# Down projection of the second FFN in Strassen's form, with its staging tiles, operand tiles and evacuations laid out anew

## The chip, the cores and the metric

The kernel runs on one core of a Trainium2 chip. The core has five engines that run side by side, each through its own list of instructions in order: TensorE (PE, matrix products, with weight loads shown as PEld), VectorE (DVE), ScalarE (ACT), GpSimd (POOL) and SyncE (SP, which only starts transfers). They share the on-chip memory SBUF; TensorE writes its sums to PSUM, from which VectorE and ScalarE read. The metric is the device time of one execution in microseconds (us), the median of several; lower is better.

## The reference

Two layers of an encoder on one sequence of 1024 tokens with 1024 channels, in float32. What matters here is the second feed-forward block and the norm behind it:

```python
def swiglu_ffn(h, w_gate, w_up, w_down):
    return (jax.nn.silu(h @ w_gate) * (h @ w_up)) @ w_down

for layer in range(DEPTH):
    h = rmsnorm(x, norm_mix_g[layer])
    ...
    x = x + y
    h = rmsnorm(x, norm_ffn_g[layer])
    x = x + swiglu_ffn(h, ffn_w_gate[layer], ffn_w_up[layer], ffn_w_down[layer])
return rmsnorm(x, final_g)
```

The hidden width is 2816, which is 22 chunks of 128. The down projection multiplies the hidden activations (2816 by 1024 tokens) by weights of 2816 by 1024.

## The kernel before

Channels lie on the 128 partitions, tokens along the free dimension, so a matmul takes 128 rows of weights and up to 512 tokens. The precision of float32 is kept by splitting each operand into a rounded part and the rest (`split`, lines 86 to 88): ScalarE casts the rounded part (L87), VectorE subtracts (L88), both from one raw tile to a "hi" and a "lo" tile. A product is then three matmuls (`mm3`, L100 to L102: hi by hi, hi by lo, lo by hi), added up in one PSUM bank.

The feed-forward block of a layer has two stages.

Gate and up (`gate_up_first`, `prep`, `gate_up_rest`, `gate_up_all`) uses Winograd's form of Strassen's products: two chunks of the hidden width, two halves of the channels and two halves of the tokens make a 2 by 2 block product with seven multiplications in place of eight. A pair of chunks has a unit for the gate and a unit for up. VectorE forms the left operands (sums of weight blocks), and the evacuations of the banks combine the products. `fin` applies silu to the gate and multiplies it with up; the four quadrants of the result leave for DRAM (`a_dram`) through GpSimd's queue of transfers.

The down projection (`down`, L737) is a plain product. It takes one half of the tokens after the other; the hidden chunks come in groups of 8, 7 and 7. For a group the activations are read back and split (`load_a`, L708), one tile of the pool tag "big" each. For each of eight output chunks a weight tile is read and split (`load_w`, L108), the products of the group are added up in one bank (`down_one`), and VectorE adds the bank to the residual `xs[m]` (L726). For layer 1 the second half of the tokens runs in blocks of 256 columns, and in its last group block after block, so that the final norm of the first block runs behind the products of the second. `final` (L876) squares and adds the channels, takes the mean by a matmul with a constant (`norm`, L531), three steps of a root, and writes eight scaled chunks out.

The order of the instructions is set by a planner: it goes through the program with a priority in the order in which the code is written, estimates when each instruction could run, and writes a list for each engine. On the chip each list runs in that order, with waits. Tiles come from pools by tag with a fixed number of buffers, and a new tile waits until an old one of its tag is no longer used. The tags that matter: "big" (28 tiles: residual and right operands), "w" (10: split weights), "raw" (3: weights as read), "cvp" (4), "cv" and "pr" (2 each), "half" (6), "ln" (4), and the PSUM tags "ps" (4 banks), "lnp" (2) and "acc" (2 in one tile). `run_behind` lets VectorE work of a generator be written between products against a budget of us.

Of the kernel before, what the change touches and what calls it, by code (L numbers as in the profile page):

```python
# [16 lines left out]
P = 128  # L17
S = 1024
# [24 lines left out]
def trunk(ctx: ExitStack, tc: tile.TileContext, xT, vecs, cw, w_in, w_out, fmap, pmap,  # L43
          wg, wu, wd, cen_m, pcnt, dft_h, dft_l, seq_h, seq_l, out):
# [20 lines left out]
    STT = nc.vector.scalar_tensor_tensor  # L65

# [15 lines left out]
    # the Newton step below leaves -2 / sqrt(v); the gains carry the -1/2  # L82
# [9 lines left out]
    def paced(ins, rows):  # L92
        """Hold ins until the products have come to that many rows."""
# [11 lines left out]
    def wtile(name):  # L105
        return arena.tile([P, 1024], F32R, tag="w", name=name, bufs=10)

    def load_w(src, cols=1024, eng=None, q=nc.sync, alloc=wtile, rows=None):  # L108
        raw = arena.tile([P, 1024], F32, tag="raw", name="raw", bufs=3)
# [10 lines left out]
    def rsqrt2(ps, e, y, v):  # L120
        """v = -2 / sqrt(ps + eps)"""
# [95 lines left out]
    def make_tables():  # L217
        # per-head feature transform folded with the head's map: [S, C, -S, -C] @ map
# [17 lines left out]
    def load_halves(src, q):  # L236
        raw = arena.tile([P, 1024], F32, tag="raw", name="raw", bufs=3)
        wh, wl = wtile("wh"), wtile("wl")
        for hs in HALVES:
            q.dma_start(raw[:, hs], src[:, hs])  # L240
        return raw, wh, wl
# [34 lines left out]
    # ---- the convolution runs behind the products: chunk 0 and part of chunk 3 on ACT and Pool,  # L276
    # the rest on DVE in what time the products leave it
# [99 lines left out]
    def tick(used):  # L377
        """After a unit of products, in which DVE has that many us of its own."""
# [41 lines left out]
    for h in range(4):  # L420
# [5 lines left out]
        # radix-4 step over the sequence: s = 256 a + b  # L426
# [15 lines left out]
    # W[c][b, (r|i), e] per head, then the 256-point transforms over b  # L442
# [86 lines left out]
    a_dram = [[dram.tile([P, S], F32, name=f"a{layer}_{f}") for f in range(NF)] for layer in range(2)]  # L529

    def norm(lo, hi):  # L531
        """-2 / rms of xs over its columns lo..hi"""
# [8 lines left out]
    # gate and up: Winograd's form of Strassen's products over two chunks of the hidden width (1, 2),  # L541
    # the two halves of the channels and the two halves of the tokens
# [5 lines left out]
    def product(ps, w, b, start, stop):  # L548
        for j in range(4):
            c = j * P  # L550
            mm3(ps, (w[:, c:c + P], w[:, TH + c:TH + c + P]), (b[j][:, :TH], b[j][:, TH:]),
                start and j == 0, stop and j == 3, skip_group_check=not start)
# [35 lines left out]
    def raw_w(src):  # L588
        raw = arena.tile([P, 1024], F32, tag="raw", name="raw", bufs=3)
# [387 lines left out]
```

## Time and profile before

| what | value |
|---|---|
| median of 3 runs | 1744.99 us (1744.05 to 1747.76) |
| span of the profiled execution | 1740.6 us |
| time of the profiled execution beyond its span | not given apart; the median of the runs is 4.4 us longer |
| mean granted TensorE clock | 0.991 |
| moved by DMA | 238.66 MB, 137 GB/s over the span |
| TensorE busy from 1204 to 1455 us (gate and up, layer 1) | 251.00 of 251 us |
| VectorE busy from 1480 to 1602 us (down, first half of the tokens) | 68.47 of 122 us |
| VectorE busy from 1602 to 1730 us (down, second half) | 73.65 of 128 us |
| GpSimd's longest group | 96 additions of 128x512, 139.3 us, all before 280 us |

The profile is one execution, recorded instruction by instruction. In its rows an engine is followed by the line of the kernel, the operation, the tile written and the tiles read, and the shape. A row of the timeline begins with the start and the duration in us, and a bracket at its end gives the time the engine was idle before it and what ended that. A row of the groups gives busy time and the mean of one instruction in ns, then the idle time ahead of the group. A row of the windows gives, for a stretch of time, how long each engine was busy in it.

### The profile page before, as it was taken

The page shows a single profiled execution, that of the slowest core. Times are in us where ns is not written, and L with a number is a line of the kernel's source. Part 1 is how long each engine was busy: PE and PEld are TensorE (multiplying, and loading weights), DVE is VectorE, ACT ScalarE, POOL GpSimd, SP SyncE. Part 2 cuts the span into 40 slices and gives each one's busy share as a digit, 9 for nine tenths or more (in the row PEclk, how much of TensorE's full clock was granted, in tenths as well). Part 3 has the DMA queues.
Part 4 walks back from the last instruction along what each step waited for, and adds up shares of the span by engine and source line. Part 5 has one row for each costly group of instructions (what it writes and reads, how often), then busy time and mean ns, then how long its engine had stood idle before and what let it go on. Part 6 is the DMA issues. An engine that isn't in the chain of part 4 may idle for free.

```text
span 1740.6 us, 22375 instructions
## 1 busy us (share of the span) xinstructions
PE 1682.0 (97%) x8318; PEld 1400.9 (80%) x8318; DVE 1245.9 (72%) x1774; ACT 692.9 (40%) x1062; POOL 276.0 (16%) x300
## 2 busy tenths in 40 slices
PE   6998899999999999999999998999999999999997
PEld 4786777777888888889998886778888888788997
DVE  8699988794577777755559768787777775545546
ACT  5455855464323232233234344553232322334223
POOL 4587764111000000000000001110000000000000
PEclk9999899999999999999999999999999999999999
DMA  5121311545633333355433425646333333644433
GB/s 188 47 97 37 135 61 46 184 142 201 232 131 122 127 109 127 116 167 174 133 109 126 152 85 182 211 163 218 133 122 127 109 127 121 204 144 160 167 122 123
DMA packets 82236, 238.66 MB, mean 137 GB/s; under 512 B 10320, under 2 KB 15696, under 8 KB 82128
## 3 DMA queue, kind: packets, MB, share of 16 engines
q1 hardware_dynamic: 65520, 186.64, 32.6%
q0 software_dynamic: 14304, 47.46, 7.2%
q10 hardware_dynamic: 2304, 3.15, 0.5%
q8 instruction: 65, 1.06, 0.3%
q14 instruction: 43, 0.35, 0.1%
HBM read 190.02 MB, written 47.19 MB: 136 GB/s over the span
## 4 chain that ended last, share of the span: by engine, by line
PE 83%; DVE 11%; DMA 3%; ACT 1%; issue 1%; SPq 0%; DVEq 0%; ACTq 0%
PE ps L100 18%; PE ps L102 18%; PE ps L101 18%; PE lnp L100 10%; PE lnp L102 10%; PE lnp L101 9%; DVE acc L313 2%; DVE acc L134 1%; DMA xin<-in_xT 1%; DMA raw<-in_wd 1%; DVE hl L88 1%; DMA raw<-in_wu 1%; DVE wl L88 1%; DVE ybl L88 0%; PE lnp L538 0%
## 5 line engine op out<-in xcount | busy, mean ns | idle before, releaser
L87 ACT CAST hl<-raw 128x512 fp32r<-128x512 f32 x264 | 161.2, 621 | 426.0 <-DVE raw L636 161.4
L100 PE MATMUL ps<-hl 128*128 128x512 f32 x704 | 277.6, 395 | 3.3 <-ACT s L617 2.8
L102 PE MATMUL ps<-hl 128*128 128x512 f32 x704 | 276.6, 393 | 0.0
L101 PE MATMUL ps<-hl 128*128 128x512 f32 x704 | 276.5, 393 | 0.0
L87 ACT CAST wh<-raw 128x896 fp32r<-128x896 f32 (+2 forms) x139 | 132.5, 953 | 243.5 <-PE ps L101 109.0
L100 PE MATMUL ps<-ahl,wh 128*128 128x256 f32 (+3 forms) x711 | 228.0, 321 | 0.5 <-ACT wh L87 0.5
L102 PE MATMUL ps<-ahl,wl 128*128 128x256 f32 (+3 forms) x711 | 227.7, 320 | 0.5 <-DVE wl L88 0.5
L101 PE MATMUL ps<-ahl,wh 128*128 128x256 f32 (+3 forms) x711 | 227.2, 320 | 0.0
L88 DVE TENSOR_TENSOR hl<-raw,hl 128x512 fp32r<-128x512 f32 x264 | 179.8, 689 | 47.9 <-ACT hl L87 43.3
L100 PE MATMUL lnp<-hl 128*128 128x512 f32 x528 | 210.2, 398 | 0.7 <-ACT s L617 0.7
L102 PE MATMUL lnp<-hl 128*128 128x512 f32 x528 | 208.1, 395 | 0.0
L101 PE MATMUL lnp<-hl 128*128 128x512 f32 x528 | 207.9, 394 | 0.0
L88 DVE TENSOR_TENSOR wl<-raw,wh 128x896 fp32r<-128x896 f32 (+2 forms) x127 | 141.6, 1116 | 48.7 <-ACT wh L87 44.3
L100 PEld LDWEIGHTS ps<-hl 128*128 128x128 f32 x704 | 132.2, 188 | 37.7 <-ACT s L617 6.9
L102 PEld LDWEIGHTS ps<-hl 128*128 128x128 f32 x704 | 132.3, 188 | 30.6
L101 PEld LDWEIGHTS ps<-hl 128*128 128x128 f32 x704 | 132.4, 188 | 29.6
L303 POOL TENSOR_TENSOR cvp<-cvp,pr 128x512 f32<-128x512 f32 x96 | 139.3, 1452 | 82.5 <-ACT pr L302 78.2
L100 PEld LDWEIGHTS ps<-ahl,wh 128*128 128x128 f32 x711 | 134.3, 189 | 11.1 <-ACT wh L87 0.9
L102 PEld LDWEIGHTS ps<-ahl,wl 128*128 128x128 f32 x711 | 134.0, 189 | 10.9 <-DVE wl L88 1.0
L101 PEld LDWEIGHTS ps<-ahl,wh 128*128 128x128 f32 x711 | 134.3, 189 | 10.2 <-issue 0.2
L653 POOL DMA_DIRECT2D a<-g x66 | 35.6, 540 | 576.6 <-DVE g L652 576.6
L100 PEld LDWEIGHTS lnp<-hl 128*128 128x128 f32 x528 | 99.5, 189 | 27.3 <-ACT s L617 4.3
(209 smaller groups left out, 3095.9 us busy)
## 6 DMA issues: line engine op xcount, KB each, us to landing
raw<-in_wg SPq DMA_DIRECT2D x66, 512.0 KB, 3.4
raw<-in_wu SPq DMA_DIRECT2D x66, 512.0 KB, 3.6
raw<-in_wd SPq DMA_DIRECT2D x72, 448.0 KB, 3.3
a<-g POOLq DMA_DIRECT2D x88, 256.0 KB, 3.1
raw<-in_wd SPq DMA_DIRECT2D x32, 512.0 KB, 3.8
p<-s POOLq DMA_DIRECT2D x44, 256.0 KB, 3.2
u<-p SPq DMA_DIRECT2D x44, 256.0 KB, 4.2
raw<-a SPq DMA_DIRECT2D x44, 256.0 KB, 3.3
```

The source lines that it names most:

```text
L87: nc.scalar.copy(hi, src)
L88: (eng or nc.vector).tensor_tensor(out=lo, in0=src, in1=hi.bitcast(F32), op=ALU.subtract)
L100: nc.tensor.matmul(ps, lh, rh, start=start, stop=False, **kw)
L101: nc.tensor.matmul(ps, lh, rl, start=False, stop=False, **kw)
L102: mm = nc.tensor.matmul(ps, ll, rh, start=False, stop=stop, **kw)
L134: TT(out=acc, in0=acc, in1=sq, op=ALU.add)
L303: nc.gpsimd.tensor_tensor(out=a, in0=a, in1=pr, op=ALU.add)
L313: STT(out=acc, in0=src, scalar=wv, in1=acc, op0=ALU.mult, op1=ALU.add)
L653: nc.gpsimd.dma_start(a_dram[layer][m][:, HALVES[t]], dst)
```

## The change

The down projection of layer 1 becomes a 2 by 2 block product of its own, over pairs of hidden chunks (11), pairs of output chunks (j = 0 to 3) and the two halves of the tokens, with seven multiplications. Layer 0 keeps the plain form.

The right operands are made once, at the end of each pair in gate and up: `combine` (called behind the up unit) reads the quadrant B11 back from DRAM, forms T1 to T4 by four additions of 128x512 on GpSimd, and stores them; B11, B21, B22 and T1 to T4 lie in `b_dram`, and B12 is no longer stored.

`down_strassen` runs two passes over blocks of pairs. Pass A has blocks of 2, 3, 3 and 3 pairs; in each block and each j five products run: A11 with B11, S2 with T2, S3 with T3, A12 with B21, A22 with T4. Pass B has blocks of 4, 3 and 4 pairs and two products: S1 with T1 and S4 with B22. Left operands are made anew for each step (`left_a`, `left_b`), one step ahead, by three additions on GpSimd each, then split by ScalarE and VectorE into tiles of tag "w". Both passes read all weights. The right operands of a block are read and split over the four steps of the block before, through the small tags "cv" and "pr", into tiles of tag "big".

Evacuations in pass A: the first product's bank is copied by ScalarE and added by GpSimd to a running sum `u2[j]` (in the first block VectorE adds the copy and the second product directly), the second product's bank is added by VectorE, two banks are copied by ScalarE and added to the residual by GpSimd (`add_pool`), one is added by VectorE. In the last block `u2[j]` is added to three quadrants, two on GpSimd and one on VectorE. In pass B VectorE adds both banks. The final norm runs over whole halves of the tokens: the first behind pass B, the second behind the end.

For the whole kernel the tags "raw" (3) and "w" (10) become one tag "w" of 13 buffers, for raw and split weights alike.

```diff
     def wtile(name):
-        return arena.tile([P, 1024], F32R, tag="w", name=name, bufs=10)
+        return arena.tile([P, 1024], F32R, tag="w", name=name, bufs=13)
+
+    def rawtile():
+        return arena.tile([P, 1024], F32, tag="w", name="raw", bufs=13)
...
+    def combine(p, g):
+        g11 = arena.tile([P, TH], F32, tag="cv", name="g11", bufs=2)
+        nc.sync.dma_start(g11, b_dram["B11"][p])
+        t1, t3 = g11, g["12"]
+        t2, t4 = (arena.tile([P, TH], F32, tag="pr", name=n, bufs=2) for n in ("t2", "t4"))
+        PTT(out=t1, in0=g["12"], in1=g11, op=ALU.subtract)
+        PTT(out=t2, in0=g["22"], in1=t1, op=ALU.subtract)
+        PTT(out=t3, in0=g["22"], in1=g["12"], op=ALU.subtract)
+        PTT(out=t4, in0=g["21"], in1=t2, op=ALU.subtract)
+        for name, src in (("T1", t1), ("T2", t2), ("T3", t3), ("T4", t4)):
+            store_b(1, name, p, src)
...
+    def load_b(names):
+        out = []
+        for n, p in names:
+            bturn[0] += 1
+            tag = ("cv", "pr")[bturn[0] % 2]
+            raw = arena.tile([P, TH], F32, tag=tag, name=tag, bufs=2)
+            nc.sync.dma_start(raw, b_dram[n][p])
+            out.append(opnd(raw, big))
+        return out
...
+    def left_a(j, p0, n):
+        a11, a12, a21, a22 = load_quads(j, p0, n)
+        w = {"A11": wopnd(a11)}
+        s3 = small("s3")[:, :n * P]
+        PTT(out=s3, in0=a11, in1=a21, op=ALU.subtract)
+        PTT(out=a21, in0=a21, in1=a22, op=ALU.add)
+        PTT(out=a21, in0=a21, in1=a11, op=ALU.subtract)
+        w["S2"], w["S3"], w["A12"], w["A22"] = wopnd(a21), wopnd(s3), wopnd(a12), wopnd(a22)
+        return w
...
+        w = left(0)
+        b = right(0, load_b(right_names(0)[1]))
+        for k in range(KD):
+            xs[k] = big(f"x{k}")
+            nc.sync.dma_start(xs[k], x_dram[layer][k])
...
+        def add_pool(dst, ps):
+            t = half("u1")
+            nc.scalar.copy(t, ps)
+            PTT(out=dst, in0=dst, in1=t, op=ALU.add)
...
+        for i, (kind, p0, n, j) in enumerate(steps):
+            if j == 0 and i + 4 < len(steps):
+                todo, got = right_names(i + 4)[1], []
+            nw = left(i + 1) if i + 1 < len(steps) else None
+            (x11, x12), (x21, x22) = x[j]
+            if kind == "a":
+                ba, bb, bd = single(), single(), single()
+                product(ba, w["A11"], b["B11"], True, True)
+                u = half("u1")
+                nc.scalar.copy(u, ba)
+                product(bb, w["S2"], b["T2"], True, True)
+                if u2[j] is None:
+                    u2[j] = arena.tile([P, TH], F32, tag="cvp", name="uu", bufs=4)
+                    TT(out=u2[j], in0=bb, in1=u, op=ALU.add)
+                else:
+                    PTT(out=u2[j], in0=u2[j], in1=u, op=ALU.add)
+                    TT(out=u2[j], in0=bb, in1=u2[j], op=ALU.add)
+                product(bd, w["S3"], b["T3"], True, True)
+                add_pool(x22, bd)
+                product(ba, w["A12"], b["B21"], False, True)
+                add_pool(x11, ba)
+                product(bd, w["A22"], b["T4"], False, True)
+                TT(out=x21, in0=bd, in1=x21, op=ALU.add)
+                if (p0, n) == blocks_a[-1]:
+                    TT(out=x21, in0=x21, in1=u2[j], op=ALU.add)
+                    for dst in (x12, x22):
+                        PTT(out=dst, in0=dst, in1=u2[j], op=ALU.add)
...
-    down(1, ([(0, TH)], [(TH, TH + 256), (TH + 256, S)]), final)
+    down_strassen(1, ((0, 2), (2, 3), (5, 3), (8, 3)), ((0, 4), (4, 3), (7, 4)), final)
```

More of the change, by code (lines that the diff above doesn't have):

```diff
@@ L236, in load_halves @@
     def load_halves(src, q):
-        raw = arena.tile([P, 1024], F32, tag="raw", name="raw", bufs=3)
+        raw = rawtile()
         wh, wl = wtile("wh"), wtile("wl")
@@ L527, in single @@
         return bank(("ps", "lnp", "ps")[turn[0] % 3])
-    a_dram = [[dram.tile([P, S], F32, name=f"a{layer}_{f}") for f in range(NF)] for layer in range(2)]
+    a_dram = [[dram.tile([P, S], F32, name=f"a0_{f}") for f in range(NF)]]
+    b_dram = {n: [dram.tile([P, TH], F32, name=f"b{n}_{p}") for p in range(NF // 2)]
+              for n in ("B11", "B21", "B22", "T1", "T2", "T3", "T4")}
     def norm(lo, hi):
@@ L548, in product @@
     def product(ps, w, b, start, stop):
-        for j in range(4):
+        n = len(b)
+        for j in range(n):
             c = j * P
             mm3(ps, (w[:, c:c + P], w[:, TH + c:TH + c + P]), (b[j][:, :TH], b[j][:, TH:]),
-                start and j == 0, stop and j == 3, skip_group_check=not start)
+                start and j == 0, stop and j == n - 1, skip_group_check=not start)
     def h_make(layer, t, bt, hf):
@@ L588, in raw_w @@
     def raw_w(src):
-        raw = arena.tile([P, 1024], F32, tag="raw", name="raw", bufs=3)
+        raw = rawtile()
         nc.sync.dma_start(raw, src)
@@ L623, in gate_up_first @@
                 TT(out=g, in0=ps, in1=g, op=ALU.mult)
[L624 removed]
+        store_b(layer, "B11", p, g)
     def prep(layer, p, wsrc, first):
@@ L696, in gate_up_all @@
             gate_up_rest(layer, p, bt, w, up, p >= nfirst, g)
+            if up and layer == 1:
+                combine(p, g)
             w = nxt
@@ L709, in load_a @@
         n = hi - lo
-        raw = arena.tile([P, 1024], F32, tag="raw", name="raw", bufs=3)
+        raw = rawtile()
         nc.sync.dma_start(raw[:, :n], a_dram[layer][f][:, lo:hi])
@@ L770, in down, with load_quads @@
         run_behind(back, 1e9)
+    def load_b(names):
[7 more added lines that the diff above has]
+        return out
+    bturn = [0]
+    def load_quads(j, p0, n):
+        out = []
+        for q in range(2):
+            raw = rawtile()
+            rv = raw.rearrange("p (a c) -> p a c", a=2)[:, :, :n * P]
+            nc.sync.dma_start(rv, wds[j, :, 2 * q:2 * q + 2, p0 * P:(p0 + n) * P])
+            out += [raw[:, :n * P], raw[:, TH:TH + n * P]]
+        return out
@@ L874, in trunk, with final @@
     gate_up_all(1, b1, NP1)
-    def final(pi, blocks):
-        for lo, hi in blocks:
-            inv = norm(lo, hi)
-            yield 6.0
-            for k in range(KD):
-                o = half("o")[:, :hi - lo]
-                STT(out=o, in0=xs[k][:, lo:hi], scalar=gneg[:, V_FIN + k:V_FIN + k + 1], in1=inv,
-                    op0=ALU.mult, op1=ALU.mult)
-                (nc.sync if k % 2 else nc.scalar).dma_start(out[k][:, lo:hi], o)
-                yield 0.65
-    down(1, ([(0, TH)], [(TH, TH + 256), (TH + 256, S)]), final)
+    def final(t):
+        hs = HALVES[t]
+        inv = norm(hs.start, hs.stop)
+        yield 6.0
+        for k in range(KD):
+            o = half("o")
+            STT(out=o, in0=xs[k][:, hs], scalar=gneg[:, V_FIN + k:V_FIN + k + 1], in1=inv,
+                op0=ALU.mult, op1=ALU.mult)
+            (nc.sync if k % 2 else nc.scalar).dma_start(out[k][:, hs], o)
+            yield 0.65
+    down_strassen(1, ((0, 2), (2, 3), (5, 3), (8, 3)), ((0, 4), (4, 3), (7, 4)), final)
 def _round_f32r(a):
@@ L947 @@
     wd = []
-    for l in range(2):
+    for l in range(1):
         parts, o = [], 0
```

70 lines of the change are left out of this document (66 added, 4 removed).

## The prediction

> **What bounds the kernel now.** I read the page first, then the stretches of TensorE in the stage that changes, then the views that show GpSimd and VectorE side by side.
>
> ```profile
> PE 1682.0 (97%) x8318; PEld 1400.9 (80%) x8318; DVE 1245.9 (72%) x1774; ACT 692.9 (40%) x1062; POOL 276.0 (16%) x300
> PE 83%; DVE 11%; DMA 3%; ACT 1%; issue 1%; SPq 0%; DVEq 0%; ACTq 0%
> ```
>
> TensorE is busy all the time and most of the chain that ended last is TensorE, so fewer products shorten the kernel, as long as nothing else takes TensorE's place. The windows give the price of a product, the timeline of TensorE gives the limits of the stage:
>
> ```profile
> 1204.00:1455.00 251.00, 251.00 (x1089) 204.19 (x1088) 186.25 (x284) 72.31 (x117) 15.11 (x28) 1.00 0.37 126
> 1500.00:1600.00 100.00, 100.00 (x435) 81.34 (x435) 54.20 (x69) 37.19 (x50) 0.00 (x0) 1.00 0.49 159
> ```
>
> ```profile
> 1478.88 0.39 PE L102 MATMUL lnp<-hl 128*128 128x512 f32 x1
> 1479.78 0.50 PE L100 MATMUL ps<-ahl,wh 128*128 128x512 f32 x1 [0.51 <-ACT wh L87]
> ...
> 1602.52 0.28 PE L100 MATMUL ps<-ahl,wh 128*128 128x256 f32 x1
> ...
> 1729.47 0.28 PE L102 MATMUL lnp<-ahl,wl 128*128 128x256 f32 x1
> ```
>
> A window row has length, then busy time and instructions of TensorE, weight load, VectorE, ScalarE and GpSimd, then clock and DMA. 435 products in 100 us is 0.230 us for 512 columns. Gate and up of layer 1 end at about 1479.3, the down projection runs to 1729.7: 250.4 us, of which the second token half, 1056 products of 256 columns, takes 127.2, or 0.120 each. So two half products cost 0.240, and cutting blocks in two costs TensorE a little as well. Behind the last product lie 10.9 us to the end of the span, 1740.6.
>
> **The change on TensorE.** Seven products for each of 11 pairs of hidden chunks and 4 pairs of output chunks (j), each of three matmuls: 7 x 11 x 4 x 3 = 924 of 512 columns, 212.5 us. Against 250.4 that is 37.9 less. This is the whole gain; all that follows gives it back.
>
> **The shared port.** The change brings GpSimd, idle in this stage, into the middle of it. Where both worked before, the conv stage shows what this does:
>
> ```profile
> 119.15 14.06 POOL L303 TENSOR_TENSOR cvp<-cvp,pr 128x512 f32<-128x512 f32 x9
> ```
>
> ```profile
> 128.78 0.42 DVE L432 TENSOR_TENSOR zs<-at 128x256 f32<-128x256 f32 x1
> 129.11 1.52 DVE L433 TENSOR_TENSOR zs<-at 128x256 f32<-128x256 f32 x1
> 130.56 1.51 DVE L434 TENSOR_TENSOR at<-at 128x256 f32<-128x256 f32 x1
> 131.99 1.50 DVE L435 TENSOR_TENSOR at<-at 128x256 f32<-128x256 f32 x1
> 133.41 0.41 DVE L436 TENSOR_TENSOR at<-zs 128x256 f32<-128x256 f32 x1
> 133.74 0.41 DVE L437 TENSOR_TENSOR at<-zs 128x256 f32<-128x256 f32 x1
> ```
>
> A VectorE operation with both inputs in SBUF takes 0.41 once GpSimd has stopped at 133.2 (starts 0.33 apart) and 1.50 while GpSimd adds (starts 1.45 apart): one of each goes by turns. So one addition of 512 columns on GpSimd takes 1.45 - 0.33 = 1.12 us from VectorE. An operation that reads PSUM keeps its 0.68 beside GpSimd:
>
> ```profile
> 112.13 1.29 POOL L303 TENSOR_TENSOR cvp<-cvp,pr 128x512 f32<-128x512 f32 x1 [2.06 <-ACT pr L302]
> ...
> 221.60 1.37 POOL L303 TENSOR_TENSOR cvp<-cvp,pr 128x512 f32<-128x512 f32 x1 [0.62 <-ACT pr L302]
> 224.03 2.39 POOL L88 TENSOR_TENSOR wl<-raw,wh 128x1024 fp32r<-128x1024 f32 x1 [1.05 <-ACT wh L87]
> ```
>
> ```profile
> 221.74 0.68 DVE L461 TENSOR_TENSOR wcl<-ps,wch 128x512 fp32r<-128x512 f32 x1
> 222.34 1.18 DVE L125 SCALAR_TENSOR_TENSOR lnb<-lnb,lna 128x512 f32<-128x512 f32 x1
> ```
>
> (The first reads PSUM. The second, starting 0.60 later, has two inputs in SBUF, finds GpSimd at work until 222.97 and ends 0.55 after that.) GpSimd takes 1.29 for 512 columns and 2.39 for 1024, so 384 take 0.28 less than 512 and 256 take 0.55 less: shares of 0.85 and 0.57. VectorE starts are 0.60 apart at 512, 0.33 at 256, so 0.47 at 384. With these an a-step (one block, one j) costs the port, in us: five left splits, 15/4 right splits for the next block, three GpSimd sums for left operands, and GpSimd's additions of evacuations.
>
> - block of 2: 5 x 0.33 + 3.75 x 0.60 + 3 x 0.57 + 2 x 1.12 = 7.85; TensorE 30 x 0.23 = 6.9
> - the next two, of 3: 5 x 0.47 + 2.25 + 3 x 0.85 + 3 x 1.12 = 10.5; TensorE 45 x 0.23 = 10.35
> - the last of 3, with two more additions of u2 on GpSimd, one on VectorE and fewer rights: 2.35 + 1.2 + 0.6 + 2.55 + 5.6 = 12.3; TensorE 10.35
> - b-steps (two left splits, 1.5, 2 and 0 rights, three GpSimd sums): 5.5, 4.7, 4.6; TensorE 5.5, 4.1, 5.5; and behind them the final norm of the first half, 15 operations, 9.5 in all.
>
> So the port becomes as full as TensorE. Taking the longer of the two by block, four steps each, and for pass B the port's sum (58.8 + 9.5 = 68.3 against 60.7), I get 27.6 + 84.0 + 49.2 + 68.3 = 229.1; the first block counts at TensorE's time, since its excess of 3.8 falls into the wait at the start. For turns that don't fit I add 3, chosen between 0 and the 20 of the third rival: 232.
>
> **The start of the stage.** Before, TensorE waits 0.5 us there. Now the first right operands are read through the four small buffers "cv" and "pr", and the last combine uses the "pr" ones for T2 and T4. I assume that a tag's buffers are handed out in the order of the program.
>
> ```profile
> 1480.90 0.68 DVE L681 TENSOR_TENSOR u<-lnp,u 128x512 f32<-128x512 f32 x1
> 1481.62 0.69 DVE L652 TENSOR_TENSOR g<-u,g 128x512 f32<-128x512 f32 x1
> ```
>
> ```profile
> a<-g POOLq DMA_DIRECT2D x88, 256.0 KB, 3.1
> raw<-a SPq DMA_DIRECT2D x44, 256.0 KB, 3.3
> out<-o ACTq DMA_DIRECT2D x4, 256.0 KB, 2.1
> ```
>
> ```profile
> L653 POOL DMA_DIRECT2D a<-g x66 | 35.6, 540 | 576.6 <-DVE g L652 576.6
> L87 ACT CAST ahl<-raw 128x512 fp32r<-128x512 f32 x44 | 27.1, 619 | 39.2 <-DMA raw<-a 35.9 <-PE ps L102 3.1
> L88 DVE TENSOR_TENSOR ahl<-raw,ahl 128x512 fp32r<-128x512 f32 x44 | 30.3, 688 | 15.2 <-ACT ahl L87 14.9
> ```
>
> From 1479.3: two VectorE operations 1.4, four GpSimd sums 5.2, two of its DMA issues 1.1, T2 landed 3.1, B11 read 3.3, cast and difference 1.3: first product at 1494.7. "pr" carries five of the ten tiles over two buffers, so its last tile comes two rounds of 3.3 + 1.3 + 0.2 later, 1504.3; the last product of the step ends at 1505.7, where 1479.3 + 6.9 would do: **19.5 lost**. Were the buffers given to whoever is ready first, it is about 1. TensorE also comes back slow from such a wait:
>
> ```profile
> 170.00:180.00 10.00, 3.70 (x15) 3.44 (x16) 10.00 (x12) 8.68 (x12) 7.41 (x5) 0.57 0.00 0
> 180.00:190.00 10.00, 6.88 (x25) 4.94 (x24) 10.00 (x14) 4.03 (x7) 6.62 (x6) 0.74 0.68 239
> ```
>
> The clock was 0.57 around a wait of 6 us and 0.74 in the 10 us after it: 0.26 x 6.88 = 1.8 lost. Stage: 232 + 19.5 + 1.8 = 253.4, 3.0 more than before.
>
> **The end.** The last half is no longer cut in two, so what follows the last product is 512 columns wide:
>
> ```profile
> L882 DVE SCALAR_TENSOR_TENSOR o<-x,gneg,v 128x512 f32<-128x512 f32 x8 | 5.5, 745 | 0.0
> L134 DVE TENSOR_TENSOR acc<-acc,sq 128x512 f32<-128x512 f32 x7 | 4.8, 686 | 0.1
> L133 ACT ACTIVATE sq<-x 128x512 f32<-128x512 f32 x7 | 4.4, 630 | 0.0
> L122 ACT ACTIVATE y<-lnp,eps 128x512 f32<-128x512 f32 x1 | 0.7, 687 | 0.0
> 1608.25 1.02 PE L538 MATMUL lnp<-acc,onesd 128*128 128x512 f32 x2
> ```
>
> Addition 0.69, square 0.63, two sums 1.3, mean 1.0, root 0.69, three steps 2.1, eight outputs 5.5, the last one out 2.5, gaps 0.5: 14.9 against 10.9, **+4.0**.
>
> **Gate and up of layer 1.** Four GpSimd sums per pair are 44 x 1.12 = 49 us of port in the 300 us of this stage, beside a VectorE that is 186 of 251 busy, 74%. Together 90%: hidden on average, behind operands made one unit (13.8 us) ahead. Between 0 and 20 I take 2, since each combine comes as a burst. One pool of 13 in place of 10 and 3 holds the same memory; TensorE waits for nothing in those 251 us; in the earlier stages another order of loads can give or take about half of the 9.4 us that TensorE is idle between 170 and 190. I take 0, with 5 either way. The additional stores and reads of T and B go beside a DMA share of 0.37: 0.
>
> **Sum.** 1740.6 + 3.0 + 4.0 + 2 = 1749.6 for the span. The median of the runs, 1744.99, is 4.4 above the span of the profiled execution, whose own time is not given apart; with it **1754**.
>
> **A rule against the row.** The Trainium skill, page "SBUF — State Buffer", section "Who interferes with whom", says that whoever issues first holds the shared port pair for the whole instruction and the other fully blocks. By it GpSimd would hold the port 1.29 where the row gives 1.12; the trace agrees on the blocking and shows 1.45 where it would have 1.29 + 0.33 = 1.62.
>
> **The rivals.** The first leans on this row:
>
> ```profile
> 1183.33 0.41 SPq L742 DMA_DIRECT2D x<-xp  x1
> ```
>
> 1. The early start (faster): buffers go to whoever is ready, and the first rights lie ready when gate and up end. -20 for the stage: 1734. For it: reads of x for this stage were issued long ahead, when gate and up had 296 us to go. Against: then reads of B11 could hold "pr" while a combine needs it.
> 2. The slack hides the port (faster): TensorE sets the pace, 212.5 in place of 232: 1734; with rival 1 1714. For it: operands lie a step ahead. Against: port and TensorE are equally full in blocks two and three, and the last has 12.3 against 10.35.
> 3. GpSimd's additions cost their full 1.29 (slower): each of the 116 that lie in blocks two to four and in pass B takes 0.17 more, 19.7 in all: 1774. It decides from the point where a port step exceeds TensorE's, 10.35 at three pairs; fixed orders, in which ScalarE waits for a GpSimd sum ahead of a copy that frees a bank, cost about the same. For it: 2.39 us behind a 1024-column addition. Against: the starts 1.45 apart.
>
> **How the numbers follow.** Forecast 1754 (1744 to 1763) 0.40; rival 3 0.22; rival 1 0.18; rival 2 0.11; both 0.05; 0.04 for a loss of over 10 in gate and up. 0.2%, 3.5 us, is about what a measurement of this kernel can tell from no change. Faster 0.34 (rivals 1 and 2 and their join), same 0.12 (the forecast's lower flank), slower 0.54. The range 1730 to 1776 takes in each rival but the join.
>
> **What would show it.** The start: TensorE idle some 15 us behind the last product of gate and up, with reads of B through "pr" late. The port: VectorE's 512-column splits well over 0.69 in pass A, and TensorE waits there for splits or copies. The end: 15 us behind the last product. It is wrong if TensorE shows no gaps in pass A, or if the reads of B11 land before 1479.

## The result: 6.2% slower, and the profile after

The changed kernel takes 1854.35 us (median of 4, 1844.04 to 1855.78), the kernel before 1744.52 beside it (1742.61 to 1747.76): a ratio of 1.062, with an interval of 1.0591 to 1.065. The forecast was 1754 with 1776 as its upper end, so the sign was right and the size was not. The profiled execution has a span of 1852.8 us, 112.2 more than before.

The first fence is from the page of the changed kernel: busy times by engine, TensorE and GpSimd in 40 slices, and the chain that ended last.

```profile
PE 1685.3 (91%) x7656; PEld 1360.2 (73%) x7656; DVE 1308.6 (71%) x1825; ACT 715.4 (39%) x1180; POOL 526.3 (28%) x513
...
PE   6898799899999999999999999999999976878785
...
POOL 4486673111000000000000011113232343655742
...
PE 36%; DVE 27%; DMA 17%; issue 10%; POOL 6%; ACT 4%; SPq 1%; DVEq 0%; POOLq 0%; ACTq 0%
```

TensorE has 662 instructions fewer and is busy 3 us longer. In the last eight slices its 9s are gone, beside digits of 2 to 7 for GpSimd, which was idle there before. The chain that ended last was 83% TensorE before and is 36% now; VectorE, transfers and GpSimd have taken its place.

To see where the 112 us arise I cut both traces at four events, read off the timeline: the last copy of the first part of gate and up of layer 1 (ScalarE, L624; L617 before), the last product with silu there (VectorE, L659; L652 before), the last product of the down projection, and the end. Later tables use the same cuts.

| stretch | before | after | more |
|---|---|---|---|
| up to the end of the first part of gate and up, layer 1 | 1171.9 | 1196.2 | 24.3 |
| rest of gate and up, layer 1 | 310.4 | 326.6 | 16.2 |
| down projection, layer 1 | 247.4 | 314.0 | 66.6 |
| behind the last product | 10.8 | 16.0 | 5.2 |

The forecast had 0, 2, 3.0 and 4.0 in these rows. So it missed in three places, the largest being the stage that the change rewrites. The window of the changed kernel for the whole down projection (length, then busy time of TensorE, weight load, VectorE, ScalarE and GpSimd, clock, DMA share):

```profile
1523.00:1837.00 314.00, 241.80 (x926) 184.07 (x926) 194.74 (x253) 120.64 (x234) 174.21 (x138) 0.90 0.49 156
```

924 products at 0.23 would be 212.5 us. TensorE is busy 241.8, 29.3 more, at a granted clock of 0.90, and it waits for 72.2. VectorE is busy for 194.7 of the 314 us, GpSimd for 174.2. The waits of TensorE, from the groups by form of the same window (busy, mean ns, then idle time ahead and what ended it):

```profile
L101 PE MATMUL ps<-hl 128*128 128x512 f32 x190 | 80.0, 421 | 40.9 <-ACT hl L88 27.3 <-DVE x L919 9.0 <-ACT u L898 4.5
...
L101 PE MATMUL lnp<-hl 128*128 128x512 f32 x118 | 51.2, 434 | 26.0 <-ACT u L882 23.6 <-DVE x L919 2.2
```

16.15 of the 27.3 us are the wait at the start of the stage. 28.1 (23.6 and 4.5) are waits for ScalarE's copies of banks (L882, L898). The timeline of one such wait, ScalarE and GpSimd first:

```profile
1603.57 1.00 POOL L836 TENSOR_TENSOR s<-raw 128x384 f32<-128x384 f32 x1 [2.32 <-DMA raw<-in_wds]
...
1605.72 0.99 POOL L838 TENSOR_TENSOR raw<-raw 128x384 f32<-128x384 f32 x1
...
1606.75 0.51 ACT L88 CAST hl<-raw 128x384 fp32r<-128x384 f32 x1 [3.72 <-POOL raw L838]
...
1608.40 0.58 ACT L882 COPY u<-lnp 128x512 f32<-128x512 f32 x1
...
1609.03 0.80 PE L101 MATMUL lnp<-hl 128*128 128x512 f32 x1 [5.31 <-ACT u L882]
1609.62 0.63 PE L102 MATMUL lnp<-hl 128*128 128x512 f32 x1
1610.05 0.63 PE L103 MATMUL lnp<-hl 128*128 128x512 f32 x1
```

A read of weights comes late, three GpSimd sums follow, ScalarE's casts of the next step's operands wait 3.72 for them, and the copy that frees the bank stands behind these casts in ScalarE's list. This looks like a clear cause. The experiments were to tell whether it is.

Two more views of the same window bear on it. The first has VectorE's splits by form: 0.80 for 384 columns and 0.93 for 512.

```profile
L89 DVE TENSOR_TENSOR hl<-raw,hl 128x384 fp32r<-128x384 f32 x56 | 44.6, 803 | 33.6 <-ACT hl L88 33.4
L89 DVE TENSOR_TENSOR hl<-cv,hl 128x512 fp32r<-128x512 f32 x38 | 35.4, 931 | 2.6 <-ACT hl L88 2.4
```

With all sums on VectorE (run e3 below) the same splits take 0.55 and 0.68:

```profile
L89 DVE TENSOR_TENSOR hl<-raw,hl 128x384 fp32r<-128x384 f32 x56 | 30.0, 552 | 1.8 <-ACT hl L88 1.7
L89 DVE TENSOR_TENSOR hl<-cv,hl 128x512 fp32r<-128x512 f32 x38 | 26.0, 684 | 2.3 <-ACT hl L88 2.2
```

The second has the waits of ScalarE's casts for GpSimd's operand sums (us in total, times, the longest): 89.8 us together.

```profile
ACT hl L88 <- POOL raw L838: 47.7, 13, 6.8
ACT hl L88 <- POOL raw L844: 27.6, 9, 5.6
ACT hl L88 <- POOL raw L846: 14.5, 7, 2.4
```

### The profile page after: what moved, and what is told of

It reads as the page before. It is cut to its first block, busy times and chain, and to the rows that moved or that the text cites. A ratio compares the mean times of both kernels' runs of the same rounds, so it can differ in the third digit from the quotient of the medians.

```text
span 1852.8 us, 21411 instructions
## 1 busy us (share of the span) xinstructions
PE 1685.3 (91%) x7656; PEld 1360.2 (73%) x7656; DVE 1308.6 (71%) x1825; ACT 715.4 (39%) x1180; POOL 526.3 (28%) x513
## 4 chain that ended last, share of the span: by engine, by line
PE 36%; DVE 27%; DMA 17%; issue 10%; POOL 6%; ACT 4%; SPq 1%; DVEq 0%; POOLq 0%; ACTq 0%
DVE hl L89 8%; PE ps L101 8%; PE ps L103 7%; PE ps L102 7%; DMA raw<-in_wg 6%; DMA raw<-in_wu 5%; PE lnp L101 4%; PE lnp L103 4%; PE lnp L102 4%; DMA raw<-in_wds 3%; ACT hl L88 2%; DVE acc L317 2%; DVE raw L643 2%; DVE raw L642 2%; DVE u L692 1%
## 5 line engine op out<-in xcount | busy, mean ns | idle before, releaser
L101 PE MATMUL ps<-hl 128*128 128x512 f32 x894 | 358.9, 402 | 62.5 <-ACT hl L88 27.3
L88 ACT CAST hl<-raw 128x512 fp32r<-128x512 f32 (+2 forms) x352 | 202.9, 593 | 544.7 <-DVE raw L643 301.8
L103 PE MATMUL ps<-hl 128*128 128x512 f32 x894 | 356.2, 399 | 1.8 <-DVE hl L89 1.7
L102 PE MATMUL ps<-hl 128*128 128x512 f32 x894 | 355.6, 398 | 0.0
L89 DVE TENSOR_TENSOR hl<-raw,hl 128x512 fp32r<-128x512 f32 (+2 forms) x352 | 249.8, 718 | 105.1 <-ACT hl L88 102.9
L101 PE MATMUL lnp<-hl 128*128 128x512 f32 x646 | 262.2, 406 | 31.3 <-ACT u L882 23.6
L103 PE MATMUL lnp<-hl 128*128 128x512 f32 x646 | 258.0, 400 | 3.6 <-DVE hl L89 3.6
L102 PE MATMUL lnp<-hl 128*128 128x512 f32 x646 | 258.2, 400 | 0.0
L101 PEld LDWEIGHTS ps<-hl 128*128 128x128 f32 x894 | 170.9, 191 | 114.9 <-ACT hl L88 54.2
L103 PEld LDWEIGHTS ps<-hl 128*128 128x128 f32 x894 | 170.4, 191 | 43.1 <-DVE hl L89 3.7
L102 PEld LDWEIGHTS ps<-hl 128*128 128x128 f32 x894 | 170.9, 191 | 39.0 <-DVE hl L89 0.9
L101 PEld LDWEIGHTS lnp<-hl 128*128 128x128 f32 x646 | 123.7, 191 | 70.8 <-ACT u L882 27.9
L103 PEld LDWEIGHTS lnp<-hl 128*128 128x128 f32 x646 | 123.9, 192 | 33.0 <-DVE hl L89 4.5
L102 PEld LDWEIGHTS lnp<-hl 128*128 128x128 f32 x646 | 124.0, 192 | 28.9 <-issue 1.0
L641 DVE TENSOR_TENSOR s<-raw 128x512 f32<-128x512 f32 x44 | 37.1, 844 | 115.1 <-DMA raw<-in_wu 60.5
L101 PE MATMUL ps<-ahl,wh 128*128 128x504 f32 (+2 forms) x358 | 115.2, 322 | 0.0
L103 PE MATMUL ps<-ahl,wl 128*128 128x504 f32 (+2 forms) x358 | 114.9, 321 | 0.0
L102 PE MATMUL ps<-ahl,wh 128*128 128x504 f32 (+2 forms) x358 | 114.7, 320 | 0.0
L88 ACT CAST wh<-raw 128x1024 fp32r<-128x1024 f32 (+2 forms) x83 | 77.6, 941 | 92.0 <-DMA raw<-in_wd 59.5
L306 ACT ACTIVATE pr<-u,cwt 128x512 f32<-128x512 f32 x96 | 69.2, 724 | 61.7 <-PE ps L103 40.3
```

What stands on the lines that cost most here:

```text
L88: nc.scalar.copy(hi, src)
L89: (eng or nc.vector).tensor_tensor(out=lo, in0=src, in1=hi.bitcast(F32), op=ALU.subtract)
L101: nc.tensor.matmul(ps, lh, rh, start=start, stop=False, **kw)
L102: nc.tensor.matmul(ps, lh, rl, start=False, stop=False, **kw)
L103: mm = nc.tensor.matmul(ps, ll, rh, start=False, stop=stop, **kw)
L306: ins = nc.scalar.activation(pr, src, AF.Copy, scale=wv)
```

## The experiments

Theories at the start: **P**, the one pool of 13 makes reads late; **G**, GpSimd's additions and the port that it shares with VectorE; **S**, the wait at the start, for buffers that the last combine holds. Later G was parted into **O** (the order: ScalarE's casts wait for GpSimd ahead of bank copies), **K** (the work itself, which slows VectorE) and **W** (only waits for GpSimd's results cost).

The runs in one table; the columns are the stretches above, and each ratio is to the kernel before on the same chip.

| run | first | gate and up | down | tail | median us | ratio (interval) |
|---|---|---|---|---|---|---|
| e1: before, one pool | 1187.3 | 310.3 | 264.6 | 12.1 | 1778.90 | 1.0208 (1.0166 to 1.0249) |
| e2: after, two pools | 1174.6 | 336.8 | 311.5 | 16.8 | 1841.50 | 1.0567 (1.0536 to 1.0598) |
| e3: after, all sums on VectorE | 1192.0 | 318.0 | 266.5 | 16.0 | 1792.03 | 1.0283 (1.0245 to 1.0321) |
| e4: after, early start | 1189.8 | 330.7 | 293.6 | 16.9 | 1837.16 | 1.0542 (1.048 to 1.0604) |
| e12: after, bank copies on VectorE | 1192.8 | 327.0 | 314.1 | 16.0 | 1851.17 | 1.0618 (1.0599 to 1.0638) |
| e5: after, banks added by VectorE | 1191.3 | 330.5 | 279.9 | 16.9 | 1821.83 | 1.0448 (1.0431 to 1.0465) |
| e11: after, operand sums on VectorE | 1192.5 | 318.1 | 286.3 | 16.9 | 1815.89 | 1.0410 (1.0395 to 1.0426) |
| e9: all remedies together | 1173.3 | 310.6 | 235.3 | 16.9 | 1737.99 | 0.9968 (0.9958 to 0.9978) |
| e13: e9, idle GpSimd additions | 1174.4 | 310.5 | 257.7 | 16.0 | 1760.39 | 1.0098 (1.0083 to 1.0112) |
| e15: e9, combine on GpSimd | 1174.2 | 334.9 | 237.3 | 16.9 | 1764.58 | 1.0120 (1.0107 to 1.0133) |
| e16: e9, one pool | 1187.3 | 318.6 | 247.3 | 16.0 | 1775.67 | 1.0176 (1.0162 to 1.0190) |
| e14: e9, norm spread out | 1172.7 | 309.0 | 235.3 | 16.2 | 1737.60 | 0.9965 (0.9952 to 0.9979) |

Each stretch is read from one profiled execution. The code up to the first cut is the same in the changed kernel, e3, e4, e5, e11 and e12, and its row still goes from 1189.8 to 1196.2, so a difference of a few us in one stretch says nothing. An edit also lets the planner write other lists, so each difference holds the edit and the new order together.

### e1 and e2: the pool alone, put in and taken out

e1 is the kernel before with the tags joined, at all places where a raw tile is allocated:

```diff
-        return arena.tile([P, 1024], F32R, tag="w", name=name, bufs=10)
+        return arena.tile([P, 1024], F32R, tag="w", name=name, bufs=13)
-        raw = arena.tile([P, 1024], F32, tag="raw", name="raw", bufs=3)
+        raw = arena.tile([P, 1024], F32, tag="w", name="raw", bufs=13)
```

> The kernel before with one tag of 13 buffers for raw and split weights, nothing else changed. If the one pool delays the reads of weights (theory P), the stages up to the end of the first part of gate and up in layer 1 lose about the 24 us that they lost in the changed kernel, and the rest nothing, since no GpSimd sum is in gate and up: about 1768. If the one pool costs nothing by itself and GpSimd's share of the port did all of it (theory G): 1745.

e2 is the changed kernel with the opposite edit in `wtile` and `rawtile`.

> The changed kernel with raw (3 buffers) and split weights (10) apart again. P: the 24 us of the early stages come back, gate and up of layer 1 loses less than half of its 18, and in the down projection the reads for the next step go out before the products release their weights, so its 315 us fall to about 275: 1780. G: only the early 24 come back: 1830.

e1 is 2% slower than before: 15.4 us in the early stages, 17.2 in the down projection. e2 gives back the early 21.6 us (1196.2 to 1174.6) and almost nothing in the down projection (311.5 against 314.0). So P holds for the early stages, and falls as the reason for the 66.6. What the pool does there is seen in the first weights of the convolution's stage. ScalarE's first cast of a weight tile of 1024 columns, in the kernel before, and the same cast in the changed one:

```profile
31.75 1.05 ACT L87 CAST wh<-raw 128x1024 fp32r<-128x1024 f32 x1 [9.36 <-DVE gxl L162]
```

```profile
54.38 3.89 ACT L88 CAST wh<-raw 128x1024 fp32r<-128x1024 f32 x4
```

and TensorE's wait for it, in the changed kernel and then in e1:

```profile
55.48 0.65 PE L101 MATMUL acc<-gxh,wh 128*128 128x512 f32 x1 [3.67 <-ACT wh L88]
...
58.14 0.80 PE L103 MATMUL acc<-gxh,wl 128*128 128x512 f32 x1 [1.58 <-DVE wl L89]
```

```profile
55.71 0.80 PE L100 MATMUL acc<-gxh,wh 128*128 128x512 f32 x1 [3.01 <-ACT wh L87]
...
58.37 0.79 PE L102 MATMUL acc<-gxh,wl 128*128 128x512 f32 x1 [1.43 <-DVE wl L88]
```

The cast is 22.6 us later, and the same two waits, 5.25 and 4.44, appear with the pool and with nothing else of the change. They are a part of the loss; the rest lies in another order of the instructions up to 166 us, which I didn't follow up.

### e3: GpSimd's sums to VectorE

```diff
-    PTT = nc.gpsimd.tensor_tensor
+    PTT = nc.vector.tensor_tensor
```

> The changed kernel with every new GpSimd sum (combine, left operands, additions of evacuations) on VectorE, pools as in the change. G: gate and up of layer 1 back near 296 us, pass A shorter by some 30 us since VectorE no longer waits for the port: about 1805. P: the late reads stay, so 1840 to 1860; if VectorE becomes the bound, above 1860.

62 us come back, 47.5 of them in the down projection and 8.6 in gate and up. GpSimd's part is the largest of all; one pool and the late start are still in this kernel.

### e4: the start

```diff
-        t2, t4 = (arena.tile([P, TH], F32, tag="pr", name=n, bufs=2) for n in ("t2", "t4"))
+        t2, t4 = half("t2"), half("t4")
...
-        w = left(0)
-        b = right(0, load_b(right_names(0)[1]))
         for k in range(KD):
             xs[k] = big(f"x{k}")
             nc.sync.dma_start(xs[k], x_dram[layer][k])
+        w = left(0)
+        b = right(0, load_b(right_names(0)[1]))
```

> The changed kernel with T2 and T4 of the combine in tag half in place of pr, and the reads of x ahead of the first rights. If the first rights wait for the buffers that the last combine holds (theory S), the gap of 16.15 us at the start of the down projection falls to 1 to 4 and the late reads of x go: 1825 to 1835. If the gap comes from the reads or casts themselves, it stays above 10 and the time is about 1850.

TensorE's timeline around the start of the stage, in the changed kernel and in e4:

```profile
1537.33 0.79 PE L101 MATMUL ps<-hl 128*128 128x512 f32 x1 [16.15 <-ACT hl L88]
```

```profile
1524.37 0.50 PE L101 MATMUL ps<-hl 128*128 128x512 f32 x1 [2.86 <-ACT u L898]
```

The wait of 16.15 is gone, the largest one left there is 2.86, and the down projection is 20.4 us shorter: S holds. (The profiled execution of e4 is 21.7 us shorter in all. The median fell by 17.2 only: it is that of two executions, 1832.83 and 1841.48.)

### e12, e5 and e11: order or work

The wait shown above suggests O. e12 takes the bank copies out of ScalarE's list and leaves GpSimd's work as it was; e5 lets VectorE add the banks straight from PSUM, without copies (one stays in the first block) and without the GpSimd additions behind them; e11 leaves the evacuations with GpSimd and moves the sums for operands (`left_a`, `left_b`, `combine`) to VectorE.

```diff
# e12
-                nc.scalar.copy(u, ba)
+                nc.vector.tensor_copy(u, ba)
...
-            nc.scalar.copy(t, ps)
+            nc.vector.tensor_copy(t, ps)
# e5
         def add_pool(dst, ps):
-            t = half("u1")
-            nc.scalar.copy(t, ps)
-            PTT(out=dst, in0=dst, in1=t, op=ALU.add)
+            TT(out=dst, in0=ps, in1=dst, op=ALU.add)
...
-                u = half("u1")
-                nc.scalar.copy(u, ba)
...
-                    PTT(out=u2[j], in0=u2[j], in1=u, op=ALU.add)
+                    TT(out=u2[j], in0=ba, in1=u2[j], op=ALU.add)
# e11, in left_a, left_b and combine
-        PTT(out=a21, in0=a21, in1=a22, op=ALU.add)
+        TT(out=a21, in0=a21, in1=a22, op=ALU.add)
```

> The changed kernel with one edit: the three bank copies of a step in pass A (u and t of add_pool) are made by VectorE, which reads PSUM, and no longer by ScalarE; GpSimd does all that it did. Theory O (order): TensorE waits in pass A because ScalarE's list has casts that wait for GpSimd's sums ahead of the copies that free banks; then the down projection, 314 us in the changed kernel, falls by some 25 to 35 us, total about 1825. Theory K (the work on the shared port fills the stage: VectorE or GpSimd at work 271 of 314 us): GpSimd's work stays and VectorE gets 44 copies x 0.68 = 30 us more, so the down projection stays within 10 us of 314 or grows, total 1845 to 1870.

> The changed kernel with all banks of pass A added by VectorE straight from PSUM: no ScalarE copies, and the 44 GpSimd additions that followed them are gone (62.7 us of GpSimd); GpSimd's sums for left operands stay. K: port work falls by about 44 x 1.12 = 49 us, and VectorE's 44 additions from PSUM cost 44 x 0.68 = 30: the down projection comes to about 290, total about 1830. O: no copy stands behind a cast that waits for GpSimd any more, so most of the gaps of pass A go: about 275, total about 1815.

> The changed kernel with the sums for left operands and those of combine on VectorE; only the evacuations stay with GpSimd. O: ScalarE's casts wait for no GpSimd sum, so down falls from 314 to about 272. K: of the sums on the port 132 become VectorE operations of 0.55 to 0.69 in place of 1.05 to 1.57 on GpSimd; 96 us of GpSimd become about 78 of VectorE, so down falls by 20 at most, to about 295. Both: gate and up of layer 1 as with all sums on VectorE, 318 in place of 326.6. Totals: O about 1804, K about 1827.

e12 gains nothing: 314.1 in place of 314.0. Its groups by form of TensorE show that the same wait has another name now, VectorE's copy (L882) in place of ScalarE's:

```profile
L101 PE MATMUL lnp<-hl 128*128 128x512 f32 x118 | 52.7, 447 | 32.7 <-DVE u L882 29.7 <-DVE x L919 2.9
```

So e12 comes out as K had expected and not as O had: moving the copies out of ScalarE's list isn't enough, although the releaser in the trace named them. (In VectorE's list they stand behind splits that wait for the same casts, so O is weakened by this run and not excluded.) The run leaves a doubt on K as well: VectorE is busy for 227.9 us in place of 194.7 (first window below), and the stage is no longer for it. So VectorE's list was not what filled the 314 us, unless the copies' new place gave back as much as the added work cost. In e5 and e11 GpSimd has less to do, and both gain, 34.1 and 27.7 us, each between what O and K expected. Windows of the down projection in e12, e5, e11 and e3:

```profile
1520.00:1834.00 314.00, 243.16 (x926) 185.44 (x926) 227.85 (x301) 96.85 (x186) 178.56 (x136) 0.90 0.49 156
```

```profile
1522.00:1802.00 280.00, 231.88 (x926) 178.13 (x926) 202.88 (x297) 100.16 (x190) 111.05 (x92) 0.93 0.54 175
```

```profile
1511.00:1797.00 286.00, 235.21 (x926) 178.90 (x926) 229.51 (x333) 121.87 (x234) 79.18 (x56) 0.94 0.53 171
```

```profile
1510.00:1776.00 266.00, 229.84 (x925) 178.62 (x926) 219.97 (x386) 122.97 (x234) 2.17 (x4) 0.94 0.56 184
```

With GpSimd busy 178, 111, 79 and 2 us the stage takes 314, 280, 286 and 266: less work on GpSimd always helps against the changed kernel, though not in proportion. VectorE alone, with all the sums, is busy 220; it does that in less time than VectorE and GpSimd together need.

### e9: all remedies

Two pools as in e2, all sums on VectorE as in e3, the start as in e4, banks added from PSUM as in e5.

> All remedies together: two pools again (raw 3, w 10), every sum on VectorE, banks added straight from PSUM, T2 and T4 of combine in tiles of tag half and the reads of x behind the first left operands' ones. Early stages as before (0 in place of +24), gate and up 318 (+8), down: start gap 2.5 in place of 16, VectorE some 215 of work beside TensorE's 213 to 225, so about 245 (-2), tail 16 (+5): about 1755. Both theories say the same here; it is run as a candidate to beat the kernel before.

It is faster than the kernel before, by 0.32% (interval 0.22 to 0.42), where 1755 was expected: gate and up come to 310.6 with the combine's sums on VectorE, no slower than before, and the down projection to 235.3, 12.1 less than before. Its window:

```profile
1484.00:1719.00 235.00, 219.08 (x915) 170.31 (x913) 214.60 (x380) 94.39 (x182) 2.16 (x4) 0.99 0.58 182
```

TensorE is busy 219.1 of 235 at a clock of 0.99, VectorE 214.6. That is near the 212.5 that the prediction set down for the products. This kernel is the base of the next runs, in which one thing at a time is put back.

### e13: GpSimd's work without anybody waiting for it

```diff
+        idle = small("idle")
+
+        def idle_add(src):
+            nc.gpsimd.tensor_tensor(out=idle[:, :TH], in0=src, in1=src, op=ALU.add)
...
                 TT(out=x21, in0=bd, in1=x21, op=ALU.add)
+                for src in (x22, x11, x21):
+                    idle_add(src)
```

> The kernel with all remedies (1738 us, down projection 235.3) with 48 additions of 128x512 put back on GpSimd, three behind each step of pass A, each of a finished residual quadrant with itself into a scratch tile that nothing reads: no engine waits for a GpSimd result, only GpSimd's work is back. K (work on the shared port): 48 x 1.12 = 54 us taken from a VectorE that has 20 us free in 235: the down projection grows by 25 to 50, total 1763 to 1788. Rival W (only waits for GpSimd's late results cost): nothing waits for them, the down projection stays below 240, total below 1743.

The stage grows by 22.4 us, 0.47 for each of the 48 additions, though no result of theirs is used. W falls for this kernel; K holds, though 22.4 is below its lower end of 25 and 1760.39 below its 1763. The groups by form show how: the splits on VectorE in e9,

```profile
L89 DVE TENSOR_TENSOR hl<-pr,hl 128x512 fp32r<-128x512 f32 x35 | 24.0, 685 | 1.0 <-ACT hl L88 0.7
L89 DVE TENSOR_TENSOR hl<-cv,hl 128x512 fp32r<-128x512 f32 x35 | 24.0, 684 | 2.2 <-ACT hl L88 2.2
```

in e13, with the additions on GpSimd,

```profile
L89 DVE TENSOR_TENSOR hl<-pr,hl 128x512 fp32r<-128x512 f32 x35 | 32.3, 923 | 1.2 <-ACT hl L88 1.2
L89 DVE TENSOR_TENSOR hl<-cv,hl 128x512 fp32r<-128x512 f32 x35 | 29.3, 836 | 1.2 <-ACT hl L88 1.2
...
L881 DVE TENSOR_TENSOR x<-ps,x 128x512 f32<-128x512 f32 x16 | 10.9, 681 | 0.0
```

```profile
L886 POOL TENSOR_TENSOR idle<-x 128x512 f32<-128x512 f32 x48 | 63.0, 1312 | 114.6 <-DVE x L881 87.8 <-DVE x L912 19.9 <-DMA cv<-bB 3.9
```

The splits, with both inputs in SBUF, go from 0.68 to 0.92 and 0.84; the additions that read PSUM (L881) stay at 0.68. The window of the stage:

```profile
1485.00:1743.00 258.00, 225.10 (x912) 170.69 (x910) 241.47 (x381) 94.77 (x183) 65.16 (x52) 0.98 0.54 166
```

VectorE is busy 241 in place of 215 us, and TensorE waits for it. Two things are not quite nothing: VectorE waits 1.0 us in all for an addition to have read its residual (L918), and the scratch tile keeps one of the four buffers of tag "ln". The planner also changed the order of some instructions of VectorE and ScalarE between the two kernels; how much that gives or takes was not parted off.

### e15 and e16: combine on GpSimd, one pool

e15 puts back the four GpSimd sums of `combine`, e16 the pool of 13.

> The kernel with all remedies, with the four sums of combine back on GpSimd (44 of 128x512 in gate and up of layer 1). K: 44 x 1.12 = 49 us of port in place of 44 x 0.69 = 30, in bursts of four that hold up the splits for the next unit: gate and up of layer 1 grows from 310.6 to about 335 (two pools with combine on GpSimd had 336.8), total about 1763. W: T1 to T4 are needed 200 us later, nothing waits, so 310.6 stays, total 1738.

> The kernel with all remedies, with one pool of 13 for raw and split weights again. If the pool's cost is its own: early stages +18 (as in the kernel before with one pool: +15, in the changed one +24), gate and up of layer 1 +8, down +10 to +17: total about 1738 + 40 = 1778. If the pool costs only beside GpSimd's work: below 1750.

e15 loses 26.6 us, 24.3 of them in gate and up. GpSimd, VectorE and TensorE around one pair, from its timeline:

```profile
1265.91 1.29 POOL L675 TENSOR_TENSOR g<-g,g 128x512 f32<-128x512 f32 x1 [2.03 <-DVE g L659]
...
1266.03 1.72 DVE L641 TENSOR_TENSOR s<-raw 128x512 f32<-128x512 f32 x1 [0.21 <-DMA raw<-in_wg]
...
1267.78 1.67 DVE L642 TENSOR_TENSOR raw<-raw 128x512 f32<-128x512 f32 x1
...
1269.98 1.17 DVE L643 TENSOR_TENSOR raw<-raw 128x512 f32<-128x512 f32 x1
...
1270.56 1.74 POOL L678 TENSOR_TENSOR t<-g,t 128x512 f32<-128x512 f32 x1
...
1271.18 1.67 DVE L650 TENSOR_TENSOR raw<-raw 128x512 f32<-128x512 f32 x1
...
1273.37 0.68 DVE L695 TENSOR_TENSOR g<-ps,u 128x512 f32<-128x512 f32 x1
...
1274.20 0.47 PE L101 MATMUL ps<-hl 128*128 128x512 f32 x1 [2.10 <-DVE g L695]
```

GpSimd's burst of four meets VectorE's burst of four sums for the next unit. Those take 1.72, 1.67, 1.17 and 1.67 in place of 0.69 each, 3.5 us more; behind them in VectorE's list stands the evacuation L695, and TensorE waits 2.10 for its bank. The trace of e15 has eight such waits of 2.10 in the eleven pairs. All of TensorE's waits in the stage come to 18.2 us, against 0.9 in e9, and 35 products behind them that start further apart give 5.6 more: 22.9 of the 24.3. No product of this stage needs T1 to T4, so W falls here too.

e16 loses 37.7 by the medians; in the profiled execution, the fastest of its four, it is 14.0, 8.0 and 12.0 in the three stretches. In gate and up the sums L641 of VectorE wait for late weights. In e9 and then in e16, in the same window:

```profile
L641 DVE TENSOR_TENSOR s<-raw 128x512 f32<-128x512 f32 x18 | 12.4, 688 | 6.6 <-DMA raw<-in_wu 6.6
```

```profile
L641 DVE TENSOR_TENSOR s<-raw 128x512 f32<-128x512 f32 x19 | 13.2, 693 | 51.5 <-DMA raw<-in_wu 36.1 <-DMA raw<-in_wg 15.4
```

51.5 us of waiting for reads in place of 6.6. The transfers are the same and take 4.0 and 4.5 us from issue to landing in place of 3.6 and 3.5, up to 1 us more; 51.5 over 19 sums is 2.7 each, so most of it must be reads that start later against their use. So the pool's cost is its own and needs no GpSimd.

### e14: the norm spread over pass B

The squares of the first half's final norm are made one by one between the steps of pass B, with the mean's product behind them and a larger budget for this work.

> The kernel with all remedies, with the final norm of the first token half spread over the steps of pass B (a square and an addition per turn, the mean's matmul later), so that TensorE doesn't wait 2.45 us for its sum and some 1 to 2 us at VectorE's bursts: 3 to 5 us less, about 1734; if the bursts are hidden anyway, 1738.

1737.60 against 1737.99: no difference. The bursts were hidden, or what they cost is paid elsewhere in pass B.

## Why the prediction was wrong, point by point

**The products on TensorE (212.5).** Right as a count, and reached nearly in e9 (219.1 busy). Mis-sized was the clock: 1.8 us were set down for one wait, and TensorE is busy 29.3 longer. By its timeline 123 products, behind the longer waits, start over 0.3 apart in place of 0.23, which is 23 of the 29.3.

**The shared port (232).** This is the step that failed: "Taking the longer of the two by block", with "For turns that don't fit I add 3". It assumes that the longer side of a block never waits for the shorter, and it sets down 3 us for all such waits. Behind the start of the stage TensorE waits 56.1 us (72.2 less 16.15) and loses the 29.3 of slower products: 85 us, where the forecast had 21.3 (232 less 212.5, and 1.8).

The price of the port was not what was set too low. GpSimd's work stands in the forecast's sums with 133 us (76 operations of 512 columns at 1.12, 48 of 384 at 0.85, 12 of 256 at 0.57). An estimate from the rows by form, the mean of each kind of VectorE operation less its mean in e3, times its count, gives about 47 us that VectorE lost in the changed kernel. The 56 additions from PSUM (38 us) were missing in the sum, but with them VectorE is busy only 194.7 of 314 us, less than the 229 to which the port was to be full.

What the runs show in its place is that the stage goes with GpSimd's work: 47.5 us for all of it (e3), 34.1 and 27.7 for parts (e5, e11), 22.4 for 48 additions whose results nobody uses (e13). By what way it does so in the changed kernel is argued, not shown. A step there is a chain of read, three sums, casts, splits, products and bank copies, and the casts wait 89.8 us for GpSimd's sums. e13 shows that slowing VectorE is enough by itself where VectorE is 91% busy. In the changed kernel it is 62% busy, and e12 gave it 33 us more work without a longer stage, which speaks for late sums there. How the 47.5 divide between the two stays open.

The signs that the prediction named all came: TensorE idle 16.15 at the start, splits over 0.69, waits for copies, 16.0 behind the last product. The kinds of loss were right, their sizes in this step were not.

**The start (19.5).** Right in mechanism and near in size. TensorE waits 16.15 where some 15 were expected, with the reads through "pr" late, and undoing it saves 20.4 in the stage. The further 4 us for the last tile through "pr" don't show as a wait: TensorE runs on without a gap until 1560.9, with other products in between.

**The end (+4.0).** Nearly right: +5.2. The rows that it named come out as expected in the timeline of the changed kernel, the two sums 1.49 for 1.3 and the outputs 5.39 for 5.5; behind the last output pass 3.4 to the end, where 2.5 was set down.

**Gate and up (+2, between 0 and 20).** The step "hidden on average" failed: +16.2, and 24.3 in e15 with nothing else changed. VectorE's 74% is an average; its four sums for the next unit and GpSimd's four meet, in eight of the eleven pairs of e15 with a wait of 2.10. Of the 16.2 in the changed kernel 8.6 go with GpSimd's sums (e3); the pool put into the best kernel costs 8.0 here (e16). With the sums on VectorE the cost is 0.2 (310.6 against 310.4). With one pool the changed kernel loses less here than with two (326.6 against 336.8 in e2): TensorE's waits are 15.8 us, 1.8 at most, at a clock of 1.00, against 19.6, 2.1 at most, at 0.98. Why they are shorter stays open.

**One pool (0, within 5).** The step "holds the same memory" was wrong as a reason. The early stages are 24.3 us longer, and 21.6 of them go again with the pools apart (e2); put into the best kernel it costs 37.7 in all. The count of buffers is the same, but a read now waits for its turn among the split tiles. The forecast looked for TensorE's waits in the kernel before, and those say nothing of reads that had been early.

**The rivals.** Rival 3 had the right sign and the right engine, GpSimd, at 1774. Its first form, a higher price of each addition, is not what the rows show (47 us lost, where even 1.12 each gives 133). Its second form, ScalarE waiting for a GpSimd sum ahead of a bank copy, is what the trace of the changed kernel shows, and in e12 the copies' move out of that list gains nothing. What waits for GpSimd's results (O and W) add to K in the changed kernel was not parted off; a kernel with GpSimd's additions there replaced by additions that nobody waits for was not run. Rival 1 was ruled out by the start. Rival 2 is what e9 shows when GpSimd has nothing to do: the slack is there, but only then.

**The stage as a sum.** From e9 to the changed kernel the down projection grows from 235.3 by 12.0 with the pool (e16), by 19.2 with the late start and the copies in the evacuation (to e3), and by 47.5 with GpSimd (to the changed kernel): 314.0. Taken out of the changed kernel one at a time the same parts read otherwise: the pool 2.5 (e2), the late start 20.4 (e4). Seven products in place of eight are worth 12 us against the 247.4 of before, not 38, with VectorE 91% busy in that stage, and the longer tail takes back 6 of them.

## What to carry to other kernels

An idle GpSimd was no free engine here: its sums of 512 columns took 1.4 to 1.6 us where VectorE needs 0.68, VectorE's operations on two SBUF inputs became slower beside them, and casts waited for them. With the sums on VectorE itself, and banks added straight from PSUM, the stage was shorter. Count the load engine by engine with all that stands in its list, look at bursts, not at averages, and follow the chain of one step before taking the longer of two sums. Tiles that are read ahead of time keep buffers of their own; and the releaser that a trace names is only the last link, so move it alone before believing it.

## What the runs showed of the hardware

**Additions that nobody needs slow VectorE.** In e13 48 GpSimd additions of 1.31 took 26.9 us more of VectorE (241.5 against 214.6), 0.56 each; the share worked out from the conv stage was 1.12. The Trainium skill, page "SBUF — State Buffer", section "Who interferes with whom", says that an operation of VectorE with at most one SBUF input, outside the modes that use two ports, doesn't contend with GpSimd; the trace agrees (L881 at 681 ns in e13). Its rule that the first to issue holds the port for the whole instruction would take up to 1.31 for each; the trace shows less. That many additions meet a PSUM read or an idle VectorE would explain it and is not shown.

**Short waits cost twice.** Behind the wait of 5.31 shown above the next products start 0.43 apart in place of 0.23, and the same holds behind shorter ones in the changed kernel:

```profile
1706.71 0.50 PE L101 MATMUL lnp<-hl 128*128 128x512 f32 x1 [4.30 <-ACT u L882]
...
1707.75 0.63 PE L102 MATMUL lnp<-hl 128*128 128x512 f32 x1
1708.17 0.63 PE L103 MATMUL lnp<-hl 128*128 128x512 f32 x1
...
1721.57 0.80 PE L101 MATMUL lnp<-hl 128*128 128x512 f32 x1 [2.61 <-ACT u L882]
```

Behind 2.61 us the products are at half pace at once, behind 4.30 only after a microsecond at full pace. The granted clock shows more: in these windows it changes at points 3.41 us apart. Two pairs of neighbouring windows between such points, each a stretch with a wait and the one behind it:

```profile
1704.31:1707.72 3.41, 1.01 (x4) 0.86 (x5) 2.45 (x4) 2.87 (x6) 2.60 (x3) 1.00 0.13 50
1707.72:1711.13 3.41, 3.41 (x9) 2.63 (x8) 3.41 (x3) 1.00 (x2) 3.33 (x3) 0.50 0.61 191
...
1717.96:1721.37 3.41, 0.99 (x5) 0.47 (x3) 1.41 (x2) 1.26 (x3) 3.34 (x3) 1.00 0.32 78
1721.37:1724.79 3.42, 3.22 (x8) 2.58 (x9) 3.42 (x3) 0.56 (x2) 2.75 (x2) 0.50 0.20 75
```

In both, TensorE is idle for 2.4 of 3.41 us, and the clock is 0.50 for the whole next stretch, whenever the wait ended. The Trainium skill, page "TensorE: Matmul & The Clock Gate", section "What's actually happening", has the array go to half rate after at least one idle window of about 3.4 us; the half rate and the length of the window agree, but here a window with 1 us of work in it was enough.
